# Strassen's products for the merge gates and the retention projection of a hybrid decoder layer, with rows kept in DRAM

## The chip, the cores and the metric

The kernel runs on one core of a Trainium2 chip. The metric is the device time of one execution in microseconds (us), given as the median of the runs. One more execution was taken with the hardware profiler; all rows of the profile come from it.

## The reference

One decoder layer on 256 tokens of width 2048, in float32. What matters here, cut from the reference:

```python
hn = rmsnorm(h, norm_mix_w[l])
q, k, v, g_ret, xr, yr, g_a, g_b = jnp.split(hn @ w_in[l], offsets, axis=-1)
...
ret = head_groupnorm(chunkwise_retention(q, k, v), ret_gn_w[l]).reshape(b, s, D_RET_V)
ret_out = jax.nn.silu(g_ret) * ret
xr = causal_dwconv(xr, rnn_conv_w[l], rnn_conv_b[l])
hr = rg_lru(xr, rg_w_a[l], rg_b_a[l], rg_w_x[l], rg_b_x[l], rg_lambda[l])
rnn_out = jax.nn.gelu(yr) * hr
merged = (jax.nn.sigmoid(g_a) * (ret_out @ w_proj_ret[l])
          + jax.nn.sigmoid(g_b) * (rnn_out @ w_proj_rnn[l]))
h = h + merged @ w_mix_out[l]
```

After it come a cross-attention over 256 memory tokens, a convolutional gated FFN of width 5632 and a last norm. All matrices of this part are 2048 x 2048 (`g_a`, `g_b`, `xr`, `yr` are column ranges of `w_in`). The tokens are the moving or the stationary side of every product, so the weights, some 400 MB with what is read twice, stream through once.

## The kernel before

**Products.** Float32 operands are split into a rounded high part and a remainder (`hi`, `lo`, type fp32r), and each product is made of three matmuls: hi x hi, lo x hi, hi x lo. Weights come in *units* of 512 rows x 512 columns (1 MB): `prefetch` (lines 241 to 288) loads a unit into `raw` (5 buffers) on SP's queue, ScalarE rounds it to `hi` (L279), VectorE takes the difference `lo` (L280); both have 3 buffers. `weight_plan` lists the blocks of columns in order, `units` hands them out and keeps two prepared ahead. Activations are split the same way and kept as tiles `s`, 8 tiles of 256 features for a vector of 2048.

**Three kinds of product.** `gemm_t` (L339) makes a block by feature: the weights are stationary, the tokens move; it uses two of the three PSUM accumulators `acc` of pool `pm`. `gemm_n` (L349 to L351) makes a block of 512 columns by token: 4 units, 96 matmuls of 128 x 512. `pair_add` (L377 to L380) makes two neighbouring blocks at once and adds them to the residual rows: the first half of the rows of both (1024) by Strassen's seven products, the other half plainly. A pair is 11 units in the order of `PAIR_UNITS`: seven products of 12 matmuls (q1 to q7) and four plain units of 24, 180 in all. It needs sums of the activations (`sums`, L413 to L432) and sums of weight blocks, which are made in `raw`, by accumulating DMAs on POOL's queue (L260) and one addition on VectorE (L284). It uses all three accumulators. Before the change, pairs are used in `w_mix_out`, `xa_w_o` and twice in each of the first two parts of `ffn_w_down`.

**Order.** `later(n, fn)` runs a helper some units later, so that its instructions stand among those of other units. The program's order is a priority; a scheduler at build time places instructions on the engines and hands out the buffers of the pools. `tmp` gives small tiles out of a pool of 10, `big` 4 KB tiles out of a pool of 25.

**The part that is changed.** After retention (two groups of four heads; `finish_head` transposes each head and splits it to a tile of `ret`) the plan goes on with block 0 of the recurrence, the four blocks of `g_a` and `w_proj_ret` in turn, blocks 1 to 3 of the recurrence, and the four blocks of `g_b` and `w_proj_rnn` in turn. A recurrent block (`recurrent`) is two `gemm_t`, for `xr` and `yr`; their accumulators are emptied by `joined` (a copy on ScalarE, L459, tile c, and an addition on VectorE, L460). The y half makes tiles y2 and yt (L809, L812) for the first accumulator before the second is emptied. Gates and the scan of the block, `recur`, run one unit into the next block: a2 (L772), the scan (L780) and rn (L786), which is split to a tile of `rnn`. `gated` makes one gate and one projection by `gemm_n` and multiplies them. `turn_merged` transposes the merged rows for `w_mix_out`.

Of the kernel before, what the change touches and what calls it, by code (L numbers as in the profile page):

```python
# [16 lines left out]
P = 128  # L17
D = 2048
S = 256
# [44 lines left out]
def weight_plan():  # L64

    w0 = "w_in"
    plan = []
    for g in range(2):
        for c in (O_Q, O_K):
            plan += [(w0, 0, NT, c + g * BW), (w0, 0, NT, O_V + g * 1024 + (c == O_K) * BW)]  # L70
        plan += [(w0, 0, NT, O_G + g * 1024 + b * BW) for b in range(2)]
    recurrent = [[(w0, 0, NT, c + b * BW) for c in (O_XR, O_YR)] for b in range(4)]
    merge = [
        [e for b in range(4) for e in ((w0, 0, NT, c + b * BW), (w, 0, NT, b * BW))]
        for c, w in ((O_GA, "w_proj_ret"), (O_GB, "w_proj_rnn"))
    ]
    plan += sum(recurrent[:1] + merge[:1] + recurrent[1:] + merge[1:], [])
    plan += residual_plan("w_mix_out")
    plan += [(w, 0, NT, b * BW) for b in range(4) for w in ("xa_w_k", "xa_w_q")]
    plan += [("xa_w_v", 0, NT, b * BW) for b in range(4)]  # L80
    plan += residual_plan("xa_w_o")
    b0 = 0
    for nb_ in FF_PARTS:
        for b in range(b0, b0 + nb_):
            plan += [("ffn_w_up", 0, NT, c + b * BW) for c in (0, FF)]
        if nb_ == 4:
            plan += [("ffn_w_down", b0 * BW, NT, b * BW, (b + 1) * BW) for b in (0, 2)]
        else:
# [61 lines left out]
def hybrid_layer(  # L150
# [22 lines left out]
    sp_ = ctx.enter_context(tc.tile_pool(name="sp", bufs=2))  # L173
    pm = ctx.enter_context(tc.tile_pool(name="pm", bufs=3, space=bass.MemoryType.PSUM))
    px = ctx.enter_context(tc.tile_pool(name="px", bufs=2, space=bass.MemoryType.PSUM))

    count = [0]

# [4 lines left out]
    def big(shape, dt=F32, s="b"):  # L183
        return bp.tile(shape, dt, tag="big", name=nm(s))

    def tmp(s="t"):
        return tp.tile([P, 2, S], F32, tag="tmp", name=nm(s))

    def acc():
        return pm.tile([P, 2, BW], F32, tag="acc", name=nm("acc"))  # L190
# [170 lines left out]
                    products_n(a[:, tt, :], st[k // 2][:, k % 2, :], hi, lo, tt, k == 0, k == nk - 1)  # L361
        return a

    def pair_add(w, row, st, ss, c0, c1, h0, h1):

        xz, yv, rw = acc(), acc(), acc()
        x, z, y, u, r, w_ = (t[:, i, :] for t in (xz, yv, rw) for i in range(2))
# [6 lines left out]
        def run(o, key, ops, parts):  # L374
            for kk, (h, l) in enumerate(ops):
                hi, lo = (t[:, kk % KH, :] for t in parts[kk // KH])
                pe.matmul(o, h, hi, start=key not in begun, stop=False, skip_group_check=True)  # L377
                begun.add(key)
                pe.matmul(o, l, hi, start=False, stop=False, skip_group_check=True)  # L379
                pe.matmul(o, h, lo, start=False, stop=kk == KC - 1, skip_group_check=True)  # L380

        def add(o, i, op=ALU.add):
            dve.tensor_tensor(out=o, in0=o, in1=i, op=op)

        for kind, parts in units(w, row, NT, c0, c1):
            if kind == "p":
                k0, (a, b), (ka, kb) = ((8, (r, w_), "rw"), (12, (r, w_), "rw"), (8, (y, u), "yu"), (12, (y, u), "yu"))[plain]
                plain += 1
                for tt, (o, key) in enumerate(((a, ka), (b, kb))):
                    cs = slice(tt * P, (tt + 1) * P)  # L390
                    run(o, key, [halves(st[(k0 + k) // 2], k % 2, cs) for k in range(KC)], parts)
            else:
                o, t, j, tt = where[kind]
                if t == "a":
                    ops = [halves(st[k], j, slice(tt * P, (tt + 1) * P)) for k in range(KC)]
                else:
                    ops = [(ss[k][:, 0, j * P : (j + 1) * P], ss[k][:, 1, j * P : (j + 1) * P]) for k in range(KC)]
                key = {"q1": "x", "q4": "u", "q6": "x", "q7": "x", "q2": "y", "q3": "r", "q5": "z"}[kind]
                run(o, key, ops, parts)
            if kind == "q1":  # L400
                add(h0[:, 0, :], x)
            elif kind == "q5":
                later(2, lambda: add(h1, rw))
                later(3, lambda: add(h1, z[:, None, :].to_broadcast([P, 2, BW])))
            elif kind == "q6":
                add(h1[:, 0, :], x, ALU.subtract)
            elif kind == "q7":
                add(h0[:, 1, :], x)
                add(h1[:, 1, :], x, ALU.subtract)
            elif kind == "q4":  # L410
                add(h0, yv)

    def sums(src, scale=None):  # L413

# [24 lines left out]
    def halves(t, j, cs=slice(0, S)):  # L439

        return t[:, j, cs], t[:, j, S + cs.start : S + cs.stop]
# [91 lines left out]
    class Pairs(list):  # L533
        def __init__(self, src, wcol):
            self.src, self.wcol, self.raw = src, wcol, []
# [215 lines left out]


    K0 = float(np.sqrt(2.0 / np.pi))
    rnn = []

    def recur(b, rgw, xr, gl):
        aa, tt_, ti = big([P, 4, S], s="aa"), big([P, 4, S], s="tt"), big([P, 4, S], s="ti")
        for j in range(4):
            t = 4 * b + j
            c1 = slice(t, t + 1)  # L760
            gp = small()
            for i in range(2):
# [4 lines left out]
            act.activation(aa[:, j, :], tr, AF.Exp, scale=neg_half_c[:, c1], bias=neg_half_c[:, c1])  # L767
            act.activation(tt_[:, j, :], tr, AF.Tanh, scale=half_c[:, c1], bias=half_c[:, c1])
        for pr in range(2):
            cs = slice(2 * pr, 2 * pr + 2)  # L770
            a2 = tmp("a2")
            dve.tensor_tensor(out=a2, in0=aa[:, cs, :], in1=aa[:, cs, :], op=ALU.mult)  # L772
            dve.scalar_tensor_tensor(
                out=tt_[:, cs, :], in0=a2, scalar=1.0, in1=tt_[:, cs, :], op0=ALU.add, op1=ALU.mult
            )
        act.activation(tt_, tt_, AF.Sqrt, scale=0.25)
        dve.scalar_tensor_tensor(out=ti, in0=ti, scalar=1.0, in1=xr, op0=ALU.add, op1=ALU.mult)
        dve.tensor_tensor(out=ti, in0=ti, in1=tt_, op=ALU.mult)
        for j in range(4):
            dve.tensor_tensor_scan(  # L780
                out=xr[:, j, :], data0=aa[:, j, :], data1=ti[:, j, :], initial=0.0, op0=ALU.mult, op1=ALU.add
            )
        for pr in range(2):
            o = tmp("rn")
            cs = slice(2 * pr, 2 * pr + 2)
            dve.tensor_tensor(out=o, in0=xr[:, cs, :], in1=gl[:, cs, :], op=ALU.mult)  # L786
            rnn.append(split_pair(o, 0.5))

    def recurrent(b):
        rgw = big([P, 2, 4, P], s="rgw")  # L790
# [36 lines left out]

    merged, merged_sums = [], []

# [19 lines left out]

# [271 lines left out]
```

## Time and profile before

| | us |
|---|---|
| median of 3 runs | 2047.0 (2045.99 to 2047.36) |
| the profiled execution | 2043.8 |
| its span, first to last instruction | 2041.9 |
| TensorE busy in the span | 2026.0 |
| VectorE busy | 1371.0 |
| ScalarE busy | 1039.3 |

In the rows below PE is TensorE, PEld its weight load, DVE VectorE, ACT ScalarE, POOL GpSimd and SP SyncE; L280 is line 280 of the kernel. A group's row gives the operation, out<-in, the count, then busy time in us and mean ns of one, and behind the bar the engine's idle time before them with what ended it. A matmul's recorded time overlaps its neighbours', so the rate is read from counts in a stretch. TensorE's granted clock is full (0.999 over the span).

### The profile page before, as it was taken

The page shows a single profiled execution, that of the slowest core. Times are in us where ns is not written, and L with a number is a line of the kernel's source. Part 1 is how long each engine was busy: PE and PEld are TensorE (multiplying, and loading weights), DVE is VectorE, ACT ScalarE, POOL GpSimd, SP SyncE. Part 2 cuts the span into 40 slices and gives each one's busy share as a digit, 9 for nine tenths or more (in the row PEclk, how much of TensorE's full clock was granted, in tenths as well). Part 3 has the DMA queues.
Part 4 walks back from the last instruction along what each step waited for, and adds up shares of the span by engine and source line. Part 5 has one row for each costly group of instructions (what it writes and reads, how often), then busy time and mean ns, then how long its engine had stood idle before and what let it go on. Part 6 is the DMA issues. An engine that isn't in the chain of part 4 may idle for free.

```text
span 2041.9 us, 25079 instructions
## 1 busy us (share of the span) xinstructions
PE 2026.0 (99%) x10436; PEld 1732.3 (85%) x10436; DVE 1371.0 (67%) x1411; ACT 1039.3 (51%) x1042; POOL 23.7 (1%) x30
## 2 busy tenths in 40 slices
PE   9999999999999999999999999999999999999998
PEld 8888888888888888888888888888878888788887
DVE  6747658544688754666555557578787787786775
ACT  6445447433466644565444445455554555554553
POOL 0000000000000000000000000000000000000000
PEclk9999999999999999999999999999999999999999
DMA  9554553555555455775545447455478555685552
GB/s 373 204 216 149 184 202 138 204 189 201 198 183 188 168 188 192 239 280 212 185 166 184 165 150 245 185 185 193 179 209 280 185 193 187 182 270 207 189 203 82
DMA packets 66209, 404.75 MB, mean 198 GB/s; under 512 B 7216, under 2 KB 11952, under 8 KB 19376
## 3 DMA queue, kind: packets, MB, share of 16 engines
q1 hardware_dynamic: 61984, 381.66, 51.2%
q0 software_dynamic: 2592, 18.88, 4.9%
q10 hardware_dynamic: 1520, 2.63, 0.4%
q8 instruction: 81, 1.33, 0.2%
q14 instruction: 32, 0.26, 0.0%
HBM read 401.04 MB, written 2.10 MB: 197 GB/s over the span
## 4 chain that ended last, share of the span: by engine, by line
PE 92%; DVE 4%; ACT 2%; DMA 1%; issue 1%; SPq 0%; POOL 0%; POOLq 0%; ACTq 0%; DVEq 0%
PE acc L339 43%; PE acc L351 12%; PE acc L349 12%; PE acc L350 12%; PE acc L380 3%; PE acc L377 3%; PE acc L379 3%; PE sm L437 2%; DVE lo L280 2%; DMA raw<-in_wall 1%; ACT hi L279 1%; PE sm L449 1%; PE sm L763 0%; DVE fv L997 0%; DVE xr L780 0%
## 5 line engine op out<-in xcount | busy, mean ns | idle before, releaser
L280 DVE TENSOR_TENSOR lo<-raw,hi 128x2048 fp32r<-128x2048 f32 (+2 forms) x378 | 855.0, 2267 | 531.5 <-ACT hi L279 530.9
L279 ACT CAST hi<-raw 128x2048 fp32r<-128x2048 f32 (+1 forms) x376 | 712.8, 1899 | 725.0 <-PE acc L350 291.5
L339 PE MATMUL acc<-s,hi 128*128 128x512 f32 x2688 | 640.1, 391 | 1.7 <-DVE hi L277 1.0
L339 PEld LDWEIGHTS acc<-s,hi 128*128 128x128 f32 x2688 | 497.1, 188 | 100.3 <-issue 2.2
L349 PE MATMUL acc<-hi,s 128*128 128x512 f32 (+1 forms) x1144 | 442.3, 387 | 0.0
L351 PE MATMUL acc<-lo,s 128*128 128x512 f32 (+1 forms) x1144 | 441.1, 386 | 0.0
L350 PE MATMUL acc<-hi,s 128*128 128x512 f32 (+1 forms) x1144 | 440.7, 385 | 0.0
L339 PEld LDWEIGHTS acc<-s,lo 128*128 128x128 f32 x2688 | 342.8, 191 | 12.2 <-DVE lo L280 1.2
L339 PE MATMUL acc<-s,lo 128*128 128x256 f32 x2688 | 350.1, 283 | 0.4 <-DVE lo L280 0.3
L351 PEld LDWEIGHTS acc<-lo,s 128*128 128x128 f32 x1144 | 215.0, 188 | 43.7 <-DVE lo L280 0.6
L349 PEld LDWEIGHTS acc<-hi,s 128*128 128x128 f32 x1144 | 215.1, 188 | 42.1 <-ACT s L470 0.3
L350 PEld LDWEIGHTS acc<-hi,s 128*128 128x128 f32 x1144 | 215.1, 188 | 42.0 <-DVE s L471 0.2
L377 PE MATMUL acc<-hi,s 128*128 128x512 f32 x264 | 103.4, 392 | 3.2 <-ACT hi L279 3.2
L380 PE MATMUL acc<-lo,s 128*128 128x512 f32 x264 | 103.7, 393 | 0.5 <-DVE lo L280 0.2
L379 PE MATMUL acc<-hi,s 128*128 128x512 f32 x264 | 103.1, 390 | 0.0
L459 ACT COPY c<-acc 128x512 f32<-128x512 f32 x84 | 48.3, 579 | 99.0 <-PE acc L339 99.0
L377 PEld LDWEIGHTS acc<-hi,s 128*128 128x128 f32 x264 | 49.6, 188 | 14.4 <-ACT hi L279 4.7
L380 PEld LDWEIGHTS acc<-lo,s 128*128 128x128 f32 x264 | 49.6, 188 | 13.4 <-DVE lo L280 3.4
L379 PEld LDWEIGHTS acc<-hi,s 128*128 128x128 f32 x264 | 49.6, 188 | 10.8 <-DVE s L471 0.7
L460 DVE TENSOR_TENSOR uz<-acc,c 128x512 f32<-128x512 f32 x44 | 30.2, 686 | 20.2 <-ACT c L459 20.2
L997 DVE SCALAR_TENSOR_TENSOR fv<-uz,pf,fv 128x255 f32<-128x255 f32 (+1 forms) x88 | 39.6, 475 | 0.0
L997 DVE SCALAR_TENSOR_TENSOR fg<-uz,pf,fg 128x255 f32<-128x255 f32 (+1 forms) x88 | 38.2, 474 | 0.0
(202 smaller groups left out, 1130.8 us busy)
## 6 DMA issues: line engine op xcount, KB each, us to landing
raw<-in_wall SPq DMA_DIRECT2D x347, 1024.0 KB, 4.8
raw<-in_wall POOLq DMA_DIRECT2D x18, 1024.0 KB, 9.2
raw<-in_wall SPq DMA_DIRECT2D x5, 512.0 KB, 8.0
nat<-in_x ACTq DMA_DIRECT2D x4, 512.0 KB, 10.0
nat<-in_x SPq DMA_DIRECT2D x4, 512.0 KB, 7.8
nat<-in_mem SPq DMA_DIRECT2D x4, 512.0 KB, 6.6
xt<-in_mem_t SPq DMA_DIRECT2D x8, 256.0 KB, 6.4
xt<-in_x_t SPq DMA_DIRECT2D x7, 256.0 KB, 7.8
```

What stands on the lines that cost most here:

```text
L279: act.copy(hi[:, a:b], raw[:, a:b])
L280: dve.tensor_tensor(out=lo[:, a:b], in0=raw[:, a:b], in1=hi[:, a:b].bitcast(F32), op=ALU.subtract)
L339: pe.matmul(a, part, sx, start=k == 0 and t == 0, stop=k == nk - 1 and t == 0, skip_group_check=True)
L349: pe.matmul(o, h, hi, start=start, stop=False)
L350: pe.matmul(o, l, hi, start=False, stop=False)
L351: pe.matmul(o, h, lo, start=False, stop=stop)
L377: pe.matmul(o, h, hi, start=key not in begun, stop=False, skip_group_check=True)
L379: pe.matmul(o, l, hi, start=False, stop=False, skip_group_check=True)
L380: pe.matmul(o, h, lo, start=False, stop=kk == KC - 1, skip_group_check=True)
L437: pe.matmul(o, a, b, start=start and i == 0, stop=stop and i == 2, skip_group_check=True)
L459: act.copy(c, a[:, :, S:BW])
L997: dve.scalar_tensor_tensor(out=y[:, s:S], in0=z[:, j, 0 : S - s], scalar=pf[:, 2 - s, t : t + 1], in1=y[:, s:S], op0=ALU.mult, op1=ALU.add,)
```

## The change

The plan now has all four recurrent blocks first, then `g_a` and `g_b` as two pairs each, `w_proj_ret` as two pairs, and `w_proj_rnn` as four plain blocks. `pair_add` is divided: `pair_products` makes the eleven units (its body is the loop of `pair_add` as before, and it calls `out` after each unit), and `pair_out` is a new user of it that puts the two blocks into fresh tiles o0 and o1. The eight gate tiles are kept (`sig`).

The sums for the gates' pairs (`xs_sums`) are made in recurrent blocks 2 and 3 by `sum_x`, which reads x by feature from DRAM again. The rows of `ret` and `rnn` are no longer split when they are made but stored to DRAM on POOL's queue (class `Kept`) and read back, split and summed where they are first used, or at a unit set by `later`.

```diff
--- before.py
+++ after.py
@@ -69,12 +69,11 @@
         for c in (O_Q, O_K):
             plan += [(w0, 0, NT, c + g * BW), (w0, 0, NT, O_V + g * 1024 + (c == O_K) * BW)]
         plan += [(w0, 0, NT, O_G + g * 1024 + b * BW) for b in range(2)]
-    recurrent = [[(w0, 0, NT, c + b * BW) for c in (O_XR, O_YR)] for b in range(4)]
-    merge = [
-        [e for b in range(4) for e in ((w0, 0, NT, c + b * BW), (w, 0, NT, b * BW))]
-        for c, w in ((O_GA, "w_proj_ret"), (O_GB, "w_proj_rnn"))
-    ]
-    plan += sum(recurrent[:1] + merge[:1] + recurrent[1:] + merge[1:], [])
+    for b in range(4):
+        plan += [(w0, 0, NT, c + b * BW) for c in (O_XR, O_YR)]
+    for w, c in ((w0, O_GA), (w0, O_GB), ("w_proj_ret", 0)):
+        plan += [(w, 0, NT, c + b * BW, c + (b + 1) * BW) for b in (0, 2)]
+    plan += [("w_proj_rnn", 0, NT, b * BW) for b in range(4)]
@@ -173,6 +172,8 @@
+    dp = ctx.enter_context(tc.tile_pool(name="dp", bufs=1, space=bass.MemoryType.DRAM))
@@ -361,42 +362,47 @@
                     products_n(a[:, tt, :], st[k // 2][:, k % 2, :], hi, lo, tt, k == 0, k == nk - 1)
         return a
 
-    def pair_add(w, row, st, ss, c0, c1, h0, h1):
...
+    def pair_products(w, row, st, ss, c0, c1, out):
...
+            out(kind, x, z, yu, rw)
+
+    def pair_add(w, row, st, ss, c0, c1, h0, h1):
+
+        def add(o, i, op=ALU.add):
+            dve.tensor_tensor(out=o, in0=o, in1=i, op=op)
+
+        def out(kind, x, z, yu, rw):
             if kind == "q1":
                 add(h0[:, 0, :], x)
             elif kind == "q5":
@@ -408,7 +414,30 @@
                 add(h0[:, 1, :], x)
                 add(h1[:, 1, :], x, ALU.subtract)
             elif kind == "q4":
-                add(h0, yv)
+                add(h0, yu)
+
+        pair_products(w, row, st, ss, c0, c1, out)
+
+    def pair_out(w, st, ss, c0):
+
+        o0, o1 = (big([P, 2, BW], s="o") for _ in range(2))
+
+        def out(kind, x, z, yu, rw):
+            if kind == "q1":
+                act.copy(o0[:, 0, :], x)
+            elif kind == "q5":
+                act.copy(o1, z[:, None, :].to_broadcast([P, 2, BW]))
+            elif kind == "q6":
+                dve.tensor_tensor(out=o1[:, 0, :], in0=o1[:, 0, :], in1=x, op=ALU.subtract)
+            elif kind == "q7":
+                act.copy(o0[:, 1, :], x)
+                dve.tensor_tensor(out=o1[:, 1, :], in0=o1[:, 1, :], in1=x, op=ALU.subtract)
+            elif kind == "q4":
+                dve.tensor_tensor(out=o1, in0=o1, in1=rw, op=ALU.add)
+                dve.tensor_tensor(out=o0, in0=o0, in1=yu, op=ALU.add)
+
+        pair_products(w, 0, st, ss, c0, c0 + BW, out)
+        return o0, o1
 
@@ -634,11 +663,35 @@
             o.append(split_pair(ta))
         return o
 
-    ret = []
+    class Kept(list):
+        def __init__(self, name, scale=None, summed=True):
+            self.rows = dp.tile([NT // 2, P, 2, S], F32, name=name)
+            self.scale, self.stored, self.sums, self.summed = scale, 0, [], summed
+
+        def store(self, t):
+
+            pool.dma_start(out=self.rows[self.stored], in_=t)
+            self.stored += 1
+
+        def __getitem__(self, i):
+            while len(self) <= i:
+                assert len(self) < self.stored
+                t = tmp("kt")
+                pool.dma_start(out=t, in_=self.rows[len(self)])
+                self.append(split_pair(t, self.scale))
+                if self.summed and len(self) <= KC:
+                    self.sums.append(sums(t, self.scale))
+            return list.__getitem__(self, i)
+
+    ret = Kept("ret")
 
     def finish_head(g, hh, raw):
         for t in transposed(raw):
-            ret.append(split_cols(t, lambda j: half_gn[:, g * 8 + hh * 2 + j : g * 8 + hh * 2 + j + 1]))
+            c = tmp("hd")
+            for j in range(2):
+                i = g * 8 + hh * 2 + j
+                act.activation(c[:, j, :], t[:, j, :], AF.Identity, scale=half_gn[:, i : i + 1])
+            ret.store(c)
 
     def retain(g, qr, kr, vs, dec, gates):
 
@@ -751,7 +804,7 @@
 
 
     K0 = float(np.sqrt(2.0 / np.pi))
-    rnn = []
+    rnn = Kept("rnn", 0.5, False)
 
     def recur(b, rgw, xr, gl):
         aa, tt_, ti = big([P, 4, S], s="aa"), big([P, 4, S], s="tt"), big([P, 4, S], s="ti")
@@ -784,7 +837,7 @@
             o = tmp("rn")
             cs = slice(2 * pr, 2 * pr + 2)
             dve.tensor_tensor(out=o, in0=xr[:, cs, :], in1=gl[:, cs, :], op=ALU.mult)
-            rnn.append(split_pair(o, 0.5))
+            rnn.store(o)
 
     def recurrent(b):
         rgw = big([P, 2, 4, P], s="rgw")
@@ -815,15 +868,15 @@
             )
         later(0, lambda a=(b, rgw, xr, gl): recur(*a))
 
-    def gated(c0, w, st, b, o):
-
-        a = gemm_n("w_in", 0, xs, NT, c0 + b * BW)
-        t = big([P, 2, BW], s="sig")
-        for tt in range(2):
-            act.activation(t[:, tt, :], a[:, tt, :], AF.Tanh, scale=half_rs0[:, tt : tt + 1])
-        z = gemm_n(w, 0, st, NT, b * BW)
-        dve.scalar_tensor_tensor(out=o, in0=t, scalar=1.0, in1=z, op0=ALU.add, op1=ALU.mult)
-        return o
+    xs_sums = []
+
+    def sum_x(i):
+
+        t = tmp("xt")
+        pool.dma_start(out=t, in_=x_t[:, 2 * i : 2 * i + 2, :])
+        for j in range(2):
+            act.activation(t[:, j, :], t[:, j, :], AF.Identity, scale=p_mix(2 * i + j))
+        xs_sums.append(sums(t))
 
     merged, merged_sums = [], []
 
@@ -837,13 +890,35 @@
             else:
                 merged.append(split_pair(t, 0.5))
 
-    recurrent(0)
-    mb = [gated(O_GA, "w_proj_ret", ret, b, big([P, 2, BW], s="mb")) for b in range(4)]
-    for b in range(1, 4):
+    for b in range(4):
+        if b == 2:
+            for i in range(KC):
+                later(2 + 3 * i, lambda i=i: sum_x(i))
         recurrent(b)
+    sig = []
+    for c in (O_GA, O_GB):
+        for b in (0, 2):
+            if c == O_GB and b == 2:
+                for i in range(KC):
+                    later(3 + 2 * i, lambda i=i: ret[i])
+            for t in pair_out("w_in", xs, xs_sums, c + b * BW):
+                for tt in range(2):
+                    act.activation(t[:, tt, :], t[:, tt, :], AF.Tanh, scale=half_rs0[:, tt : tt + 1])
+                sig.append(t)
+
+    def gated(t, z):
+        dve.scalar_tensor_tensor(out=t, in0=t, scalar=1.0, in1=z, op0=ALU.add, op1=ALU.mult)
+
+    for b in (0, 2):
+        if b == 2:
+            for i in range(KC):
+                later(8 + i, lambda i=i: rnn[i])
+        for i, z in enumerate(pair_out("w_proj_ret", ret, ret.sums, b * BW)):
+            gated(sig[b + i], z)
     for b in range(4):
-        m = gated(O_GB, "w_proj_rnn", rnn, b, big([P, 2, BW], s="m"))
-        dve.tensor_add(m, m, mb[b])
+        m = sig[4 + b]
+        gated(m, gemm_n("w_proj_rnn", 0, rnn, NT, b * BW))
+        dve.tensor_add(m, m, sig[b])
         for pr in range(2):
             later(pr, lambda m=m, pr=pr: turn_merged(m, pr))
```

More of the change, by code (lines that the diff above doesn't have):

```diff
@@ L362, in gemm_n @@
         return a
-    def pair_add(w, row, st, ss, c0, c1, h0, h1):
-        xz, yv, rw = acc(), acc(), acc()
-        x, z, y, u, r, w_ = (t[:, i, :] for t in (xz, yv, rw) for i in range(2))
+    def pair_products(w, row, st, ss, c0, c1, out):
+        xz, yu, rw = acc(), acc(), acc()
+        x, z, y, u, r, w_ = (t[:, i, :] for t in (xz, yu, rw) for i in range(2))
         where = {
@@ L372, in pair_add, with run @@
         begun, plain = set(), 0
-        def run(o, key, ops, parts):
+        def run(o, ops, parts):
             for kk, (h, l) in enumerate(ops):
                 hi, lo = (t[:, kk % KH, :] for t in parts[kk // KH])
[L377 to L383, printed above, removed]
+                pe.matmul(o[0], h, hi, start=o[1] not in begun, stop=False, skip_group_check=True)
+                begun.add(o[1])
+                pe.matmul(o[0], l, hi, start=False, stop=False, skip_group_check=True)
+                pe.matmul(o[0], h, lo, start=False, stop=kk == KC - 1, skip_group_check=True)
+        names = {"q1": "x", "q2": "y", "q3": "r", "q4": "u", "q5": "z", "q6": "x", "q7": "x"}
         for kind, parts in units(w, row, NT, c0, c1):
             if kind == "p":
-                k0, (a, b), (ka, kb) = ((8, (r, w_), "rw"), (12, (r, w_), "rw"), (8, (y, u), "yu"), (12, (y, u), "yu"))[plain]
+                k0 = 8 + 4 * (plain % 2)
+                for tt, o in enumerate((((r, "r"), (w_, "w")), ((y, "y"), (u, "u")))[plain // 2]):
+                    cs = slice(tt * P, (tt + 1) * P)
+                    run(o, [halves(st[(k0 + k) // 2], k % 2, cs) for k in range(KC)], parts)
                 plain += 1
-                for tt, (o, key) in enumerate(((a, ka), (b, kb))):
-                    cs = slice(tt * P, (tt + 1) * P)
-                    run(o, key, [halves(st[(k0 + k) // 2], k % 2, cs) for k in range(KC)], parts)
             else:
@@ L397, in pair_add @@
                     ops = [(ss[k][:, 0, j * P : (j + 1) * P], ss[k][:, 1, j * P : (j + 1) * P]) for k in range(KC)]
-                key = {"q1": "x", "q4": "u", "q6": "x", "q7": "x", "q2": "y", "q3": "r", "q5": "z"}[kind]
-                run(o, key, ops, parts)
+                run((o, names[kind]), ops, parts)
+            out(kind, x, z, yu, rw)
[3 more added lines that the diff above has]
+        def out(kind, x, z, yu, rw):
             if kind == "q1":
```

## The prediction

> **What bounds the kernel now.** I read the page's head, the chain that ended last and the costliest groups first, then a table by stage, then the order of single instructions in one recurrent block.
>
> ```profile
> span 2041.9 us, 25079 instructions
> ...
> PE 2026.0 (99%) x10436; PEld 1732.3 (85%) x10436; DVE 1371.0 (67%) x1411; ACT 1039.3 (51%) x1042; POOL 23.7 (1%) x30
> ...
> PE 92%; DVE 4%; ACT 2%; DMA 1%; issue 1%; SPq 0%; POOL 0%; POOLq 0%; ACTq 0%; DVEq 0%
> ...
> L280 DVE TENSOR_TENSOR lo<-raw,hi 128x2048 fp32r<-128x2048 f32 (+2 forms) x378 | 855.0, 2267 | 531.5 <-ACT hi L279 530.9
> L279 ACT CAST hi<-raw 128x2048 fp32r<-128x2048 f32 (+1 forms) x376 | 712.8, 1899 | 725.0 <-PE acc L350 291.5
> ```
>
> TensorE is busy for 99% of the span and is 92% of the chain. So a removed matmul counts in full, unless its place is taken by a wait. Each weight unit also costs VectorE 2.27 us (lo) and ScalarE 1.90 us (hi). The next table cuts the span by stage (columns: stretch, length, PE, PEld, DVE, ACT and POOL busy with instruction counts, clock, DMA share, GB/s).
>
> ```profile
> 216.30:281.40 65.10, 65.10 (x289) 53.91 (x288) 41.06 (x53) 26.35 (x20) 0.00 (x0) 1.00 0.52 186
> 513.20:557.60 44.40, 44.40 (x257) 39.30 (x256) 28.17 (x27) 19.69 (x16) 0.00 (x0) 1.00 0.60 212
> 557.60:606.40 48.80, 48.49 (x274) 42.37 (x273) 41.00 (x48) 31.73 (x41) 0.00 (x0) 1.00 0.47 174
> 606.40:655.60 49.20, 48.51 (x274) 42.38 (x273) 41.09 (x48) 32.88 (x42) 0.00 (x0) 1.00 0.52 191
> 557.60:583.40 25.80, 25.80 (x146) 22.73 (x145) 19.26 (x22) 19.53 (x28) 0.00 (x0) 1.00 0.44 159
> 335.30:513.00 177.70, 177.70 (x787) 147.00 (x785) 92.83 (x61) 80.03 (x70) 0.00 (x0) 1.00 0.53 188
> 836.60:878.70 42.10, 42.10 (x189) 34.42 (x189) 33.06 (x22) 24.61 (x21) 1.75 (x2) 1.00 0.95 303
> 1485.10:1570.10 85.00, 83.10 (x362) 67.01 (x361) 69.16 (x51) 45.52 (x31) 4.36 (x5) 1.00 0.76 229
> ```
>
> The first row is three plain blocks of 96 matmuls: 65.1/288 = 0.226 us per matmul, so a plain pair of blocks (192) takes 43.4 us. The last two are pairs already done by seven products: 180 matmuls, 40.7 us at that rate. The first of them takes 42.1 us with some transposes in it, the last two together 85.0 us instead of 81.4. So this kind of pair runs near TensorE's rate, and two of them behind a busy VectorE lose 3.6 us. Rows two to four are the recurrent blocks 1 to 3: the first, with no recur before it, takes 44.4 us for 256 matmuls (5.55 us a unit), those with the previous block's recur 48.8 and 49.2 us at 41 us of VectorE.
>
> **What is removed.** Six plain pairs become pairs of seven products: 6 x 12 = 72 matmuls x 0.226 = **16.3 us** off TensorE, all of it on the path.
>
> **What the new pairs add.** Each has 11 units instead of 8 and one addition in raw.
>
> ```profile
> L284 DVE TENSOR_TENSOR raw<-raw,raw 128x2048 f32<-128x2048 f32 x6 | 13.7, 2285 | 0.1
> L383 DVE TENSOR_TENSOR nat<-nat,acc 128x512 f32<-128x512 f32 (+1 forms) x42 | 37.7, 909 | 0.2
> L468 DVE TENSOR_TENSOR s<-mt,s 128x512 fp32r<-128x512 f32 x4 | 2.7, 683 | 0.0
> L426 DVE TENSOR_TENSOR ss<-sm,ss 128x512 fp32r<-128x512 f32 x8 | 5.5, 686 | 2.1 <-ACT ss L425 2.1
> L420 DVE TENSOR_TENSOR sm<-fo 128x128 f32<-128x128 f32 x8 | 2.3, 287 | 0.1
> L493 ACT ACTIVATE s<-xt,pb 128x256 fp32r<-128x256 f32 x16 | 6.9, 501 | 0.0
> ```
>
> VectorE per new pair: 11 x 2.27 + 2.29 + four additions out of PSUM at about 0.91 = 30.9 us against 40.7 us of TensorE, which the pair at 1485 shows can be covered (69.2 of 85.0 for two). It is not covered where other work meets it. The first gate pair meets the evacuation of the last recurrent block and its recur: 41.0 us of VectorE in a block of which 18.1 is weight splitting (8 x 2.27), so about 23 us of other work, a good half of it late; 31 + 13 = 44 us in 40.7. I take 3.5 us, the loss of the two pairs at 1485. The last gate pair also splits four tiles of ret and makes their sums (4 x (0.68 + 0.69 + 4 x 0.29) = 10 us, much of it early): 1.0. In the first projection pair ret[4] and ret[5] are split only after o0 has its buffer, so behind one hi (1.90) and one lo (2.27): 1.5, since q3 can run meanwhile. The other three: 0.4 each. Together 7.2. The plain stretch that they replace was not perfect either: 177.7 us for 768 matmuls (173.6) and 19 small ones; over all replaced blocks I take 2.0 back. **Net +5.2 us.**
>
> The six pairs also bring 18 accumulating DMAs, 885 ns each on POOL, of a kind that the existing pairs hide. Reloading ret and rnn from DRAM I cost at nothing: between the last recur and the last gate pair no other tile of the small pool is made, so the loads can be issued many units early. If that cover is gone, each waits one landing, 6.4 us below.
>
> **What the new order costs.** Here the change has its price, and it starts from how buffers of the small pool (`tmp`, 10) are handed out. Rows of ScalarE around the end of recurrent block 1, and the same copy in the FFN:
>
> ```profile
> 555.08 0.59 ACT L459 COPY c<-acc 128x512 f32<-128x512 f32 x1 [2.76 <-PE acc L339]
> ...
> 558.70 0.63 ACT L809 ACTIVATE y<-yz 128x512 f32<-128x512 f32 x1
> 561.54 1.91 ACT L279 CAST hi<-raw 128x2048 fp32r<-128x2048 f32 x1 [2.21 <-issue]
> 563.35 0.63 ACT L812 ACTIVATE yt<-y 128x512 f32<-128x512 f32 x1
> 563.88 0.57 ACT L459 COPY c<-acc 128x512 f32<-128x512 f32 x1
> ```
>
> ```profile
> 1482.58 0.59 ACT L459 COPY c<-acc 128x512 f32<-128x512 f32 x1 [2.76 <-PE acc L339]
> 1486.70 0.56 ACT L459 COPY c<-acc 128x512 f32<-128x512 f32 x1
> ```
>
> In the FFN the second copy out of PSUM follows the first after 4.1 us. Behind the y half of a recurrent block it comes after 8.8 us, right behind yt, though ScalarE sat idle for 2.21 us before. The program makes the tiles in the order c, y2, yt, then the second c. So a tile of this pool gets its buffer only after those made before it, and a late one holds up the copies that free PSUM. In recurrent block 2 the tiles before the copies are recur's rn:
>
> ```profile
> 571.46 0.69 DVE L772 TENSOR_TENSOR a<-aa 128x512 f32<-128x512 f32 x1 [0.65 <-ACT aa L767]
> ...
> 575.52 0.68 DVE L772 TENSOR_TENSOR a<-aa 128x512 f32<-128x512 f32 x1
> ...
> 583.14 1.27 DVE L786 TENSOR_TENSOR rn<-xr,gl 128x512 f32<-128x512 f32 x2
> ```
>
> ```profile
> 569.46 0.63 ACT L812 ACTIVATE yt<-y 128x512 f32<-128x512 f32 x1 [0.37 <-DVE y L811]
> ...
> 585.51 1.05 ACT L459 COPY c<-acc 128x512 f32<-128x512 f32 x2
> ```
>
> The x half's matmuls end at 583.4 (row 557.60:583.40) and both copies come together at 585.5, behind rn. TensorE hardly waits: it can do the first half of up to three units of the next gemm on the free accumulator (there are three hi/lo buffers), 3 x 2.8 = 8.3 us.
>
> The change puts `sum_x(0)` between rn and these copies. It makes xt, which waits for a DMA, and then a tile of sums; both stand ahead of the copies. The DMA is issued on POOL behind two stores of rn, which wait for VectorE. Prices:
>
> ```profile
> L260 POOL DMA_DIRECT2D raw<-in_wall x18: 862/873/1053, 830.3 to 1813.2; - x18
> ...
> raw<-in_wall POOLq DMA_DIRECT2D x18, 1024.0 KB, 9.2
> ...
> xt<-in_mem_t SPq DMA_DIRECT2D x8, 256.0 KB, 6.4
> ...
> out<-nat SPq DMA_DIRECT2D x6, 256.0 KB, 2.8
> ```
>
> A plain 256 KB load on POOL's queue is not in the trace. Bounds: 2.8 us (a store of the size at the quiet end) and 9.2 us (1 MB accumulated on POOL's queue). I take 6.4, a load of the same layout and size beside the weight stream. Then in block 2: rn ends at 584.4, two store issues 1.7, landing 6.4, two scalings 1.0, copy and addition 1.3 = 594.9. TensorE has work until 583.4 + 8.3 = 591.6: **3.3 us** of stall. In block 3 `sum_x(2)` stands between yt (569.46 on block 2's clock) and a2: 569.5 + 0.9 + 6.4 + 1.0 = 577.7, and the second a2 at 578.9 instead of 575.5, so rn 3.4 us later, and `sum_x(3)` behind it again: **6.7 us**. With 9.2 us the two give 6.1 + 12.3 = 18.4, with 2.8 us nothing. `sum_x(1)` has room.
>
> Block 1 now has recur(0) in it and block 0's y copies come behind four new hd tiles: 2.0 (0 to 4; if the transposes come early it is nothing). Below nothing is excluded, since recur is moved and not removed. VectorE also loses rn's split per block; it is not what the copies wait for.
>
> [...]
>
> **Sum.** -16.3 + 5.2 + 3.3 + 6.7 + 2.0 = +0.9 us. The profiled execution took 2043.8 us (span 2041.9 and 1.9 around it); it becomes 2044.7. The median shown, 2047.0, lies 3.2 above it, so I predict **2047.9 us**: the saving is eaten by new waits in the recurrent blocks. The case's own range is 2044 to 2051.
>
> **Rivals.** *Early landing, faster.* Loads land near 2.8 us, or the sums don't stand ahead of the copies, and the two stalls vanish: -16.3 + 5.2 + 0 + 1 = -10.1, so 2036.9. For it: the pairs of before, and TensorE's 8.3 us of reserve. Against: the 8.8 us between the copies. *Late landing, slower.* With 9.2 us: -16.3 + 5.2 + 18.4 + 2.5 = +9.8, so 2056.8. It decides from about 8 us on, where the sum passes +4 (each further us costs twice in block 3, once in block 2). For it: POOL's queue is slower than SP's for 1 MB (9.2). Against: a quarter of the bytes, no accumulation. [...] *VectorE bound, slower.* If the first gate pair and the last give no overlap for 44 us and 41 us of VectorE, blocks 2 and 3 at 41 us plus 4 x 1.9 us of sums also push: 3 + 3 + 4 more, about 2055. *The products are not fewer:* then TensorE keeps 10436 instructions; by the code that is all but excluded.
>
> **Chances.** A measurement of this kernel can tell about 0.2%, 4.1 us. Forecast 0.28; early landing 0.33; late landing 0.22; VectorE bound 0.16; products 0.01 (counted as slower). Faster 0.33, same 0.28, slower 0.39. The range goes from the faster case's 2036.9, less 1, to the late landing with a little VectorE load on top: 2036 to 2060.
>
> **What would show it.** TensorE's instructions fall by 72. The six pairs lie near 41 us each. Blocks 2 and 3 are longer than 48.8 and 49.2 by 3 and 7 us, their x copies follow the sums' first subtraction, and xt lands 6 us after its issue on POOL. Wrong, if the blocks keep their length (early landing), if an accumulating DMA waits behind a reload on POOL's queue, or if the pairs take over 43.4 us.

## The result, and the profile after

The kernel after takes 2064.6 us (median of 4 runs, 2062.3 to 2069.5), the kernel before 2046.5 in the same session: ratio 1.0092, 95% interval 1.0073 to 1.0111. It is slower by 18 us. The profiled execution took 2064.8 us against 2043.8, so the two traces differ by 21.0 us. The forecast was 2047.9, and 2064.6 lies above the whole range, 2036 to 2060.

The page's head after (busy time, share, instructions):

```profile
span 2063.0 us, 25251 instructions
...
PE 2021.7 (98%) x10364; PEld 1723.4 (84%) x10364; DVE 1454.1 (70%) x1491; ACT 1095.8 (53%) x1102; POOL 59.5 (3%) x84
```

TensorE has 72 instructions fewer, as it should, but only 4.3 us less busy time, and it idles for 41.3 us of the span instead of 15.9. The stages show where (stretch, length, PE, PEld, DVE, ACT and POOL busy, clock, DMA share, GB/s). Before, the whole changed stretch and its plain blocks:

```profile
281.40:836.60 555.20, 554.10 (x2726) 469.00 (x2725) 348.37 (x340) 283.17 (x284) 2.86 (x2) 1.00 0.52 185
...
335.20:513.10 177.90, 177.90 (x787) 147.20 (x786) 92.83 (x61) 80.13 (x70) 0.00 (x0) 1.00 0.53 189
655.60:836.60 181.00, 180.99 (x810) 149.51 (x810) 104.81 (x86) 88.39 (x81) 1.05 (x1) 1.00 0.52 182
```

After: the four recurrent blocks and the rest; then recurrent blocks 1 to 3 and the six pairs, each with the gap behind it:

```profile
280.30:482.80 202.50, 199.25 (x1150) 175.24 (x1149) 163.30 (x223) 131.01 (x170) 10.40 (x16) 1.00 0.54 190
482.80:856.40 373.60, 351.85 (x1507) 284.99 (x1506) 271.39 (x206) 208.79 (x175) 25.93 (x36) 0.97 0.74 232
...
334.20:384.40 50.20, 48.53 (x275) 42.37 (x274) 41.27 (x48) 31.82 (x44) 2.17 (x4) 1.00 0.59 221
384.40:433.10 48.70, 48.67 (x275) 42.37 (x275) 42.61 (x56) 34.79 (x46) 2.75 (x5) 1.00 0.59 205
433.10:482.80 49.70, 48.23 (x274) 42.23 (x273) 41.71 (x55) 34.79 (x46) 2.54 (x4) 1.00 0.51 173
482.80:537.10 54.30, 47.06 (x199) 37.56 (x197) 45.66 (x51) 38.32 (x40) 7.17 (x11) 0.97 0.73 224
537.10:582.20 45.10, 43.07 (x181) 34.82 (x181) 31.35 (x19) 25.38 (x18) 2.62 (x3) 0.96 0.82 245
582.20:627.20 45.00, 43.00 (x181) 34.75 (x181) 30.68 (x17) 25.27 (x18) 2.60 (x3) 0.96 0.79 232
627.20:670.80 43.60, 41.39 (x181) 33.61 (x181) 35.31 (x25) 29.42 (x26) 7.19 (x11) 1.00 0.88 279
670.80:723.80 53.00, 45.96 (x180) 36.18 (x180) 32.96 (x21) 27.32 (x22) 3.77 (x5) 0.90 0.73 217
723.80:766.40 42.60, 41.38 (x180) 33.63 (x180) 35.40 (x26) 26.36 (x22) 1.70 (x2) 1.00 0.82 246
```

The recurrent blocks 2 and 3 are as long as before (48.8 and 49.2). The pairs are not near the 41 us that were forecast: they take 42.6 to 54.3 us with their gaps, where a plain pair of blocks takes 43.4. VectorE is busy for 31 of 45 us in the second and third, so it is not full. The whole stretch took 576.1 us (202.5 + 373.6) instead of 555.2, 20.9 us more, which is the difference of the traces. What TensorE waited for between 482.8 and 766.5 (line waited for: us in total, times, longest):

```profile
PE acc L378 <- DVE o L434: 11.8, 5, 3.2
PE acc L378 <- ACT s L496: 3.0, 1, 3.0
PE acc L381 <- DVE lo L281: 2.7, 1, 2.7
PE acc L380 <- DVE s L497: 1.6, 1, 1.6
PE acc L378 <- ACT o L429: 1.3, 1, 1.3
PE acc L350 <- DVE o L434: 1.2, 1, 1.2
```

13.0 of 21.6 us are one wait at each of the six pairs' ends, for `pair_out`'s subtraction of q7 (L434). The order of single instructions at the end of the second pair (lines of the kernel after: L433 copies q7, L434 subtracts it, L436 adds rw, L437 adds the third accumulator, yu; L378 and L381 are matmuls):

```profile
577.27 1.92 ACT L280 CAST hi<-raw 128x2048 fp32r<-128x2048 f32 x1 [0.80 <-PE acc L380]
...
579.09 0.57 ACT L433 COPY o<-acc 128x512 f32<-128x512 f32 x1
...
579.22 2.29 DVE L281 TENSOR_TENSOR lo<-raw,hi 128x2048 fp32r<-128x2048 f32 x1 [0.42 <-ACT hi L280]
...
579.79 0.39 PE L381 MATMUL acc<-lo,s 128*128 128x512 f32 x1
...
581.42 0.68 DVE L434 TENSOR_TENSOR o<-o,acc 128x512 f32<-128x512 f32 x1
...
582.02 1.21 DVE L437 TENSOR_TENSOR o<-o,acc 128x1024 f32<-128x1024 f32 x1
...
582.16 0.50 PE L378 MATMUL acc<-hi,s 128*128 128x512 f32 x1 [1.98 <-DVE o L434]
...
583.15 1.21 DVE L436 TENSOR_TENSOR o<-o,acc 128x1024 f32<-128x1024 f32 x1
...
584.00 0.63 PE L381 MATMUL acc<-lo,s 128*128 128x512 f32 x1
```

q7's copy waits behind a hi, its subtraction behind a lo, and only then can the next pair's q1 start. The additions that empty the other two accumulators (L437, L436) come still later: at 579.79, when the pair's last matmul is issued, all three accumulators are still to be read. The last row shows the second part of the price. A matmul now takes 0.63 instead of 0.39, because the granted clock fell behind the gap (behind the second and the third pair):

```profile
582.20:586.20 4.00, 4.00 (x11) 3.13 (x12) 4.00 (x3) 2.56 (x4) 0.00 (x0) 0.57 0.97 219
627.20:631.20 4.00, 4.00 (x18) 3.31 (x19) 4.00 (x3) 2.92 (x5) 0.00 (x0) 1.00 0.98 213
```

In 4 us there are 11 matmuls at clock 0.57 and 18 at 1.00: 7 x 0.226 = 1.6 us are lost where it falls. Behind the third pair's gap it did not fall; the last section sets the two side by side.

### The profile page after: what moved, and what is told of

Read it like the earlier page. It is cut to its first block, busy times and chain, and to the rows that moved or that the text cites. A ratio compares the mean times of both kernels' runs of the same rounds, so it can differ in the third digit from the quotient of the medians.

```text
span 2063.0 us, 25251 instructions
## 1 busy us (share of the span) xinstructions
PE 2021.7 (98%) x10364; PEld 1723.4 (84%) x10364; DVE 1454.1 (70%) x1491; ACT 1095.8 (53%) x1102; POOL 59.5 (3%) x84
## 4 chain that ended last, share of the span: by engine, by line
PE 61%; DVE 3%; DMA 2%; ACT 1%; issue 1%; POOL 0%; POOLq 0%; ACTq 0%; DVEq 0%
PE acc L340 32%; PE acc L350 5%; PE acc L352 5%; PE acc L351 5%; PE acc L381 4%; PE acc L380 4%; PE acc L378 4%; DMA raw<-in_wall 2%; DVE lo L281 2%; PE sm L466 1%; ACT hi L280 1%; PE sm L478 1%; DVE fv L1072 0%; DVE s L500 0%; DVE raw L285 0%
## 5 line engine op out<-in xcount | busy, mean ns | idle before, releaser
L281 DVE TENSOR_TENSOR lo<-raw,hi 128x2048 fp32r<-128x2048 f32 (+1 forms) x396 | 895.5, 2268 | 477.2 <-ACT hi L280 469.4
L280 ACT CAST hi<-raw 128x2048 fp32r<-128x2048 f32 (+1 forms) x394 | 747.2, 1900 | 689.3 <-issue 172.0
L350 PE MATMUL acc<-hi,s 128*128 128x512 f32 (+1 forms) x760 | 292.6, 385 | 1.2 <-DVE o L434 1.2
L352 PE MATMUL acc<-lo,s 128*128 128x512 f32 (+1 forms) x760 | 291.2, 383 | 0.0
L351 PE MATMUL acc<-hi,s 128*128 128x512 f32 (+1 forms) x760 | 290.9, 383 | 0.0
L378 PE MATMUL acc<-hi,s 128*128 128x512 f32 x528 | 210.1, 398 | 18.0 <-DVE o L434 11.8
L381 PE MATMUL acc<-lo,s 128*128 128x512 f32 x528 | 209.0, 396 | 2.1 <-DVE lo L281 1.9
L380 PE MATMUL acc<-hi,s 128*128 128x512 f32 x528 | 208.9, 396 | 1.6 <-DVE s L497 1.6
L350 PEld LDWEIGHTS acc<-hi,s 128*128 128x128 f32 x760 | 142.9, 188 | 28.6 <-DVE o L434 1.6
L352 PEld LDWEIGHTS acc<-lo,s 128*128 128x128 f32 x760 | 142.8, 188 | 28.5 <-DVE lo L281 0.2
L351 PEld LDWEIGHTS acc<-hi,s 128*128 128x128 f32 x760 | 143.0, 188 | 27.2 <-DVE s L500 0.2
L378 PEld LDWEIGHTS acc<-hi,s 128*128 128x128 f32 x528 | 100.8, 191 | 42.5 <-DVE o L434 13.9
L381 PEld LDWEIGHTS acc<-lo,s 128*128 128x128 f32 x528 | 100.8, 191 | 25.7 <-DVE lo L281 4.6
L380 PEld LDWEIGHTS acc<-hi,s 128*128 128x128 f32 x528 | 100.9, 191 | 23.7 <-DVE s L497 2.3
L381 PE MATMUL acc<-lo,ss 128*128 128x512 f32 x192 | 75.7, 394 | 2.7 <-DVE lo L281 2.7
L378 PE MATMUL acc<-hi,ss 128*128 128x512 f32 x192 | 76.1, 396 | 1.4 <-ACT o L429 1.3
L380 PE MATMUL acc<-hi,ss 128*128 128x512 f32 x192 | 75.4, 393 | 0.0
```

The lines of the kernel that those rows point to most:

```text
L280: act.copy(hi[:, a:b], raw[:, a:b])
L281: dve.tensor_tensor(out=lo[:, a:b], in0=raw[:, a:b], in1=hi[:, a:b].bitcast(F32), op=ALU.subtract)
L350: pe.matmul(o, h, hi, start=start, stop=False)
L351: pe.matmul(o, l, hi, start=False, stop=False)
L352: pe.matmul(o, h, lo, start=False, stop=stop)
L378: pe.matmul(o[0], h, hi, start=o[1] not in begun, stop=False, skip_group_check=True)
```

## The experiments

All ratios are to the kernel before, timed on the same chip. All kernels but those that say otherwise change `pair_out` of the kernel after.

**1. Subtraction from SBUF.**

```diff
-                dve.tensor_tensor(out=o1[:, 1, :], in0=o1[:, 1, :], in1=x, op=ALU.subtract)
+                dve.tensor_tensor(out=o1[:, 1, :], in0=o1[:, 1, :], in1=o0[:, 1, :], op=ALU.subtract)
```

> One operand changes: the subtraction of q7 out of o1 reads q7's copy in o0 (SBUF) and no longer the accumulator. So the accumulator is free once ScalarE's copy is done. Theory A (the loss sits at the ends of the six pairs, where TensorE waits 13.9 us in all for this subtraction, and in the low clock behind these waits, some 6 to 9 us): the six waits shrink to about 1 us each or less, and the time falls from 2064.6 to 2045 to 2052. Rival B (VectorE's load in the pairs is the bound, the subtraction is only where it shows): the same idle time comes back under the name of lo, and the time stays within 4 us of 2064.6.

Measured: 2066.7 us, 1.0097 [1.0080, 1.0114]. No gain: theory A in this form missed. The waits of its trace:

```profile
PE acc L378 <- DVE o L436: 15.4, 5, 4.2
```

The next q1 no longer waits, but the plain unit behind it, which writes the accumulator of rw, waits for L436, the addition of rw. The wait has only passed from one accumulator to another.

**2. q7's copy on VectorE.**

```diff
-                act.copy(o0[:, 1, :], x)
+                dve.tensor_copy(o0[:, 1, :], x)
```

> q7's copy out of the accumulator is made by VectorE instead of ScalarE, so that both reads are on one engine, as in the pairs of before; VectorE gets 6 x 0.6 = 4 us more work. Theory A, in the form that the price lies in the chain hi, copy on ScalarE, lo, subtraction on VectorE: one engine's queue of lo, copy, subtraction is left, the six waits fall from 13.9 us to some 4 to 7, and the time to 2050 to 2057. Rival B (VectorE bound): more VectorE work, so 2065 to 2070.

Measured: 2058.2 us, 1.0057 [1.0042, 1.0072]. The time is a little above theory A's 2050 to 2057. The waits for L434 and L436 fall to 5.9 us together. VectorE got more work and the kernel became faster, so its load is not the bound (rival B).

**3. ret[4] and ret[5] early,** in the last gate pair.

```diff
                     later(3 + 2 * i, lambda i=i: ret[i])
+                later(10, lambda: ret[5])
```

> ret[4] and ret[5] are loaded and split in the last gate pair instead of in the first projection pair. Theory A: the two waits of 3.2 and 2.2 us in the first projection pair go, and with them the low clock right behind (some 2 to 4 us): 2055 to 2060. Rival C (that pair's 50.2 us come from its start, behind the second gate tiles' tanh and the wait for the subtraction): less than 2 us, 2063 to 2066.

Measured: 2058.8 us, 1.0060 [1.0045, 1.0075]: the waits for L496 and L497 are gone, as theory A said.

**4 and 10. The change's order with plain blocks.** Reloads and sums stay. In 4 the reload of rnn stands where it stood, in 10 five units earlier (the last two lines).

```diff
-        pair_products(w, 0, st, ss, c0, c0 + BW, out)
+        for i, o in enumerate((o0, o1)):
+            a = gemm_n(w, 0, st, NT, c0 + i * BW)
+            act.copy(o, a)
...
-                later(8 + i, lambda i=i: rnn[i])
+                later(3 + i, lambda i=i: rnn[i])
```

> The order of the change, the rows kept in DRAM and the sums stay, but the six pairs are made as plain blocks, two gemm_n and a copy each (72 matmuls more, as before). Theory A (the loss is in the pairs themselves): near the time before plus the recurrent blocks' 3 to 4 us and a little for ret[4], 2048 to 2053. Rival D (the new order, the loads on GpSimd's queue and the sums bear the loss, 16.3 us of saving eaten): 2075 to 2081, as after plus the saving that is given up.

> The order of the change with plain blocks, as before, but rnn's rows are reloaded and split five units earlier, since their split came late there and cost 3.4 and 2.4 us at the start of w_proj_rnn. Theory A: that wait goes and what is left over before is the recurrent blocks' 3.5 us: 2047 to 2050. Against it the kernel with the pairs repaired (2041.3) then shows what 72 matmuls fewer are worth net: 6 to 9 of 16.3 us. Rival D (order and reloads cost more than that): 2053 or more.

Measured: 2054.7 us, 1.0048 [1.0033, 1.0063] for 4, above theory A's 2048 to 2053; it has two waits for rnn's split (3.2 and 1.8 us in its trace) that come from my edit, since plain blocks have fewer units for `later` to count. Without them 10 gives 2046.3 us, 1.0001 [0.9991, 1.0011]. So the new order, the rows in DRAM and the sums cost nothing that can be measured; rival D is out. Its stages:

```profile
280.20:482.60 202.40, 199.14 (x1149) 175.15 (x1148) 163.26 (x223) 131.03 (x170) 9.51 (x15) 1.00 0.53 191
482.60:837.60 355.00, 355.00 (x1579) 293.70 (x1578) 197.98 (x158) 175.09 (x151) 10.77 (x19) 1.00 0.58 208
```

**7. Filler matmuls** behind each pair, into a small accumulator that nobody reads.

```diff
         pair_products(w, 0, st, ss, c0, c0 + BW, out)
+        f = small()
+        for _ in range(9):
+            pe.matmul(f.rearrange("p a n -> p (a n)"), st[0][:, 0, 0:P], st[0][:, 0, :], start=True, stop=True)
```

> The kernel after, with nine matmuls of 0.23 us behind each pair that multiply a split tile into a small accumulator which nobody reads; the build puts them where it expects TensorE to idle (first gate pair, ends of four pairs, the wait for ret[4]). The waits themselves stay. Theory E (about 9 of the 18 us are matmuls at the low clock behind a wait): the granted clock stays at 1.00 there and the time falls by 5 to 9 us, to 2056 to 2060. Rival F (the low clock is not a matter of the idle time before it, or the fillers only push the next pair back): 2063 to 2070.

Measured: 2062.8 us, 1.0084 [1.0067, 1.0101]. Its interval overlaps that of the kernel after, so the 2 us between them are no gain that is shown; theory E said 5 to 9. But the clock did what theory E said (two ends, each with the 4 us behind it: 579 with filler, 623 where the build put none):

```profile
579.30:582.00 2.70, 2.70 (x13) 2.17 (x13) 2.70 (x3) 1.92 (x1) 0.30 (x1) 1.00 0.92 173
581.80:585.80 4.00, 4.00 (x19) 3.31 (x19) 4.00 (x3) 2.97 (x6) 0.00 (x0) 1.00 1.00 225
622.80:625.10 2.30, 0.35 (x2) 0.00 (x0) 2.30 (x3) 1.90 (x1) 0.23 (x1) 1.00 0.87 175
625.10:629.10 4.00, 3.96 (x11) 3.10 (x12) 4.00 (x3) 2.56 (x4) 0.00 (x0) 0.58 0.99 213
```

So the clock stayed full where the idle time was filled: 1.00 over 581.80 to 585.80, where the kernel after has 0.57 over 582.20 to 586.20. The mean granted clock of the profiled execution is 0.996, against 0.994 in the kernel after and 0.999 before. Another end without filler, at 536, kept its clock (1.00 over 538.30 to 542.30) all the same, behind 2.3 us of idle time (2.80 - 0.48 in 535.60 to 538.40); why is not shown. The sum was off because the fillers take an estimated 54 x 0.226 = 12.2 us and the waits in this trace still add to 12.1: 24.3 us where there were 21.6. And the end at 623, which kept its clock in the kernel after (the row at 627.20), lost it here.

**9. rw added early, alone.**

```diff
                 act.copy(o1, z[:, None, :].to_broadcast([P, 2, BW]))
+                later(2, lambda: dve.tensor_tensor(out=o1, in0=o1, in1=rw, op=ALU.add))
...
-                dve.tensor_tensor(out=o1, in0=o1, in1=rw, op=ALU.add)
```

> The kernel after, with only the one edit that o1 += rw is made two units behind q5; q7's copy stays on ScalarE. It was not run alone before: the copy on VectorE gave 6.4 us, both together 16. Theory A2 (whichever read frees the first accumulator last is the wait, so each edit alone leaves the other's chain): the chain hi, copy on ScalarE, lo, subtraction on VectorE still ends last, the six waits of 2 us and the clock behind them stay: 2060 to 2065. Rival G (the chain at the end was o1 += rw all along, and the copy's engine hardly matters): 2049 to 2054.

Measured: 2049.0 us, 1.0009 [0.9998, 1.0020]. This one edit takes off nearly all of the loss. Theory A2 missed, and rival G had the time right (2049 to 2054). Its trace is of an execution of 2055.2 us, the longest of the ten, so the order of instructions is read from it and not the time. The order at the same place (L430 is the early addition of rw, L434 and L435 are the former L433 and L434):

```profile
565.86 1.21 DVE L430 TENSOR_TENSOR o<-o,acc 128x1024 f32<-128x1024 f32 x1
...
577.13 0.59 ACT L434 COPY o<-acc 128x512 f32<-128x512 f32 x1
...
577.26 2.29 DVE L281 TENSOR_TENSOR lo<-raw,hi 128x2048 fp32r<-128x2048 f32 x1 [0.42 <-ACT hi L280]
...
577.79 0.39 PE L381 MATMUL acc<-lo,s 128*128 128x512 f32 x1
...
578.01 0.39 PE L378 MATMUL acc<-hi,s 128*128 128x512 f32 x1
...
579.47 0.68 DVE L435 TENSOR_TENSOR o<-o,acc 128x512 f32<-128x512 f32 x1
```

The chain hi, copy, lo, subtraction is as long as ever, and the subtraction still reads the old x at 579.47. But the next pair's q1 began at 578.01: it has another accumulator. Of the three, x's is still read and q4 is just finishing in the third, so it is the one that rw left at 567.1, 10.7 us before the pair's last matmul. So that chain costs only while no other accumulator is free, as in experiment 2, where making it shorter took off 6 us. The cause of the price is that `pair_out` gave back none of its three accumulators until its last product was done.

**5, 6 and 8. Edits together.** 5 is 2 with 9; 6 adds 3; 8 adds 1.

> As the run with q7's copy on VectorE, and in addition the sum o1 += rw is made two units behind q5 (where the pairs of before make it) instead of behind q4. Theory A2 (at a pair's end three reads out of the accumulators stand behind one another and behind lo on VectorE, and whichever frees the next pair's first accumulator last is the wait; in the run with the subtraction from SBUF it was o1 += rw): with that read gone from the end the six waits are under 0.7 us each, and the time is 2 to 4 us below the 2058.2 of the copy alone: 2054 to 2057. Rival B (VectorE's load in the pairs as such): no change, 2057 to 2060.

> Both edits to the pairs' ends, and ret[4] and ret[5] split in the last gate pair. Theory A2: the parts add up; the 5 to 7 us around the first projection pair's start go as well, 2047 to 2051, about the time before, with the first gate pair's 4 us and the recurrent blocks' 3.5 us left. Rival B: the last gate pair takes the splitting of two more tiles on VectorE, and gives back what the next pair gains: 2054 to 2058.

> As the kernel with all three edits, and q7's subtraction reads the copy in o0 instead of the accumulator, so one read out of the accumulator is left behind q7. Theory A2: 0 to 2 us below the kernel with three edits, 2046 to 2051. Rival B: no difference beyond 1 us.

Measured: 2048.7 us, 1.0014 [1.0004, 1.0023] for 5; 2041.7, 0.9982 [0.9973, 0.9991] for 6; 2041.3, 0.9978 [0.9969, 0.9988] for 8. All three came out below what theory A2 expected (2054 to 2057, 2047 to 2051 and 2046 to 2051), since it took the early rw for the smaller part. 5 is no better than 9, so the engine of the copy is of no account once rw leaves early. 6 and 8 are some 4 us faster than the kernel before. The stage of the pairs and the waits of 6:

```profile
482.90:833.10 350.20, 343.87 (x1507) 280.17 (x1506) 274.37 (x212) 205.15 (x169) 25.94 (x36) 1.00 0.79 247
```

```profile
PE acc L381 <- DVE lo L281: 3.1, 2, 2.7
PE acc L380 <- DVE s L497: 1.7, 1, 1.7
PE acc L378 <- ACT o L429: 1.3, 1, 1.3
```

**11 and 12. The last recur later.** Kernel 8, with the last `recur` four units later (11) or seven (12), against the waits that are left in the first gate pair.

```diff
-        later(0, lambda a=(b, rgw, xr, gl): recur(*a))
+        later(4 if b == 3 else 0, lambda a=(b, rgw, xr, gl): recur(*a))
```

> The repaired kernel (all edits), with the last recur begun four units later, so that its 16 small matmuls, scan and rn lie in the later units of the first gate pair. Theory H (that pair's waits of 1.4 and 2.9 us at q6 and behind come from the scan and rn that stand ahead of lo on VectorE, with the low clock behind them): they shrink to under 1.5 us together, 2036 to 2039. Rival I (VectorE is full for the whole pair, 43 of 51 us, and the wait only moves to a later unit or to the next pair): 2040 to 2043.

> As the run before it, with the last recur seven units later, so that its scan falls at the pair's end and in the next pair. Theory H: 2035 to 2039, the second gate pair takes it up, since it has 10 us of free VectorE. Rival I: the scan meets the reads out of the accumulators at the pair's end, whose wait comes back with 2 to 4 us: 2042 to 2046.

Measured: 2043.1 us, 0.9986 [0.9976, 0.9995] and 2053.0, 1.0032 [1.0020, 1.0044]. In 11 the two old waits (for lo, and for the copy of z, L429) are gone and a new one of 5.6 us for lo stands in the second gate pair: the recur took its wait with it, as rival I said. In 12 lo is waited for 9.1 us, and a small matmul of the recur waits 3.5. Its 2053.0 us are above what theory H and rival I expected, and these waits are not the one for the reads out of the accumulators that rival I named. Where the recur would fit is not found.

## Why the prediction was wrong

The rows above give a ledger by its own terms. The plain reference for the pairs is experiment 10.

| term | predicted | measured | from |
|---|---|---|---|
| 72 matmuls | -16.3 | -16.3 | count of instructions |
| what the pairs lose | +7.2 | +34.9 | 373.6 - (355.0 - 16.3) |
| plain blocks replaced | -2.0 | -3.9 | 355.0 - (177.9 + 181.0) |
| recurrent block 1 | +2.0 | +5.8 | 50.2 - 44.4 |
| block 2, sums | +3.3 | -0.1 | 48.7 - 48.8 |
| block 3, sums | +6.7 | +0.5 | 49.7 - 49.2 |
| sum | +0.9 | +20.9 | traces: 21.0 |

The third row holds two things. The prediction took 2.0 us back as a loss of the plain blocks, but its own row shows none: 787 matmuls x 0.226 = 177.9 us, and the stretch took 177.7. The -3.9 measured fits the 18 small matmuls of a recur that left this stretch (1597 matmuls in the rows of before, 1579 in experiment 10; 18 x 0.226 = 4.1).

**The pairs: the step that failed.** The prediction worked out VectorE's load per pair (30.9 us; the second and third gate pair show 31.4 and 30.7) and concluded from the existing pairs that 40.7 us of TensorE cover it. The load was right and the conclusion was not: five of the six pairs take over 43.4 us with their gaps, which the prediction itself had named as a sign of being wrong. The existing pairs add rw two and z three units behind q5; `pair_out` reads rw only behind q4, the last product. The code showed it, but the prediction asked only how long the reads take, not which accumulator is free when the next pair begins. The 34.9 us divide by rows: 21.8 are idle time (373.6 - 351.9), 8.0 are the clock, as TensorE is busy for 351.85 us here and 343.87 in experiment 6 with the same 1507 instructions, and 5.1 remain (experiment 6 has them too: 343.9 busy where 355.0 - 16.3 = 338.7 would do). Of these 5.1 an estimated 1.3 to 1.8 are low clock that experiment 6 still has among the pairs: its mean granted clock, to two digits, is 0.99 over 482.80 to 743.10, a loss of more than 0.005 x 260.3, and 1.00 over the whole stage, one of less than 0.005 x 350.2. The rest stays open. In experiment 6 the pairs lose 11.5 (350.2 - 338.7), so 4.8 of the 16.3 us are kept. Experiment 9 shows the accumulators as the cause, 3 the split of ret, and 7, with the last section, that the low clock goes with the idle time ahead of it. The clock was in no term: the trace of before had 0.999, and behind its first 20 us no wait of TensorE above 0.9 us that tested it.

**ret[4] and ret[5]** were foreseen at 1.5 us and waited for 4.6 (3.0 + 1.6), with clock 0.90 over that pair. **The first gate pair** was foreseen at 3.5 for a busy VectorE; its own waits for lo and the copy of z are 4.0 us, and both are gone in experiment 11 with the recur, so this was right in kind and size. The low clock behind them (0.97 over the pair) was not in it.

**The sums in blocks 2 and 3** did not stall. Loads on POOL's queue and the stores of rn in block 2 (start, us):

```profile
393.89 0.55 POOL L876 DMA_DIRECT2D xt<-in_x_t  x1 [30.32 <-DVE yz L489]
409.44 1.14 POOL L673 DMA_DIRECT2D rnn<-rn  x2 [15.00 <-DVE rn L839]
...
```

```profile
ret<-hd POOLq DMA_DIRECT2D x8, 256.0 KB, 6.8
rnn<-rn POOLq DMA_DIRECT2D x8, 256.0 KB, 2.6
kt<-ret POOLq DMA_DIRECT2D x8, 256.0 KB, 11.0
kt<-rnn POOLq DMA_DIRECT2D x8, 256.0 KB, 7.3
...
xt<-in_x_t POOLq DMA_DIRECT2D x4, 256.0 KB, 5.3
```

The landing was sized well (6.4 taken, 5.3 measured). But the load was issued 15.5 us before the stores of rn that the prediction put ahead of it. So the wrong step is "a tile of this pool gets its buffer only after those made before it": the order of making the tiles did not bind the order of issue here. The 8.8 us between the two copies, from which the rule was drawn, had another cause, which no run here settles.

**Block 1** was right in kind: recur(0) lies in it with 18 more matmuls (275 against 257) and one wait of 1.7 us. Most of its 5.8 is the work that left the plain stretch.

Of the rivals, early landing had the order right (blocks 2 and 3 keep their length), and the repaired kernel 8 comes to 2041.3 where that rival gave 2036.9. VectorE as the bound had the sign for the wrong reason. None had a wait at every pair's end, and that is why the range was too low. Two of the rivals' figures do not follow from their own terms either: at three times each further us the late landing passes +4 at about 7.5 us and not 8, and VectorE as the bound adds 10 to 2047.9, about 2058 and not 2055. Neither decides anything here.

## What to carry to other kernels

When a product is taken from one place to another, compare when each of its accumulators is given back, not only how long its reads take: with three in use and three in all, one read that was done well before the last matmul of each of six pairs (10.7 us at the end shown), and no longer behind it, took off 15.6 us (2064.6 to 2049.0). A short wait of TensorE is to be costed with the slow matmuls behind it, here 1.6 us behind a wait of 2.0. Where a wait only changes its name, as in experiment 1, the resource behind it is shared, and one should ask which of its users comes free first.

## What the runs showed of the hardware

A gap of 1.98 us in TensorE's work before 582.16 was followed by a lower granted clock (0.57 over the next 4 us); one of 1.99 us before 627.16 was not (1.00). Among the pairs of the kernel after the clock is at half for 3.41 us from 514.46, 538.35, 582.72 and 671.47 each, and for 6.83 from 678.30. The distances of these times (23.89, 44.37, 88.75 and 6.83 us) are 7, 13, 26 and 2 times 3.413; the times on that grid are called marks here. The stretch before a mark and the one behind it, at the second pair's end, and then the stretch before a mark at the third's:

```profile
579.31:582.72 3.41, 1.43 (x6) 0.86 (x5) 3.41 (x3) 2.25 (x2) 0.74 (x1) 1.00 1.01 240
582.72:586.13 3.41, 3.41 (x9) 2.62 (x8) 3.41 (x3) 2.56 (x4) 0.00 (x0) 0.50 1.00 226
623.68:627.09 3.41, 1.50 (x7) 0.92 (x5) 3.41 (x4) 2.88 (x3) 0.87 (x1) 1.00 1.02 317
```

TensorE idled for 3.41 - 1.43 = 1.98 us in the first and for 1.91 in the third, behind which the clock stayed full. With that trace cut at all its marks from 20 us to 2052, five stretches at full clock have 1.98 us or more of idle time (1.98, 2.19, 2.20, 2.72 and 2.92), and each is followed by half clock; no other is, and the most idle time among the others is the 1.91. So the length of the gap does not tell the two ends apart (1.98 and 1.99 us), and the idle time between two marks does, by 0.07 us in this one trace. And the same 256 KB on POOL's queue landed in 2.6 us as a store of rn, in 6.8 as a store of hd and in 11.0 as a load of ret (medians of eight each).
